# Coarser chunks in the first tile and finer chunks in the last tile of a split SiLU-and-multiply kernel

## The chip, the cores and the metric

One Trainium2 chip, one core. The metric is the device time of one execution in microseconds (us). The profile's span is about 2 us shorter than this time (468.4 against 470.3 us for the kernel before) and is what all positions below refer to.

## The reference

```python
batch, seq, dim = (32, 512, 2048)            # x: float32, 134.22 MB
x1, x2 = x[..., :1024], x[..., 1024:]
out = x1 * (1 / (1 + np.exp(-x1))) * x2      # float32, 67.11 MB
```

There are 16,384 rows. Each is read once (8 KB) and gives an output row of 4 KB.

## The kernel before

The rows are cut into 16 tiles of 128 partitions x 8 rows. Each tile is loaded by one 8 MB DMA from the SP queue, ScalarE (ACT) writes SiLU of the left half into an output tile, VectorE (DVE) multiplies the right half into it, and the output is stored from the ACT queue. There are two input and two output buffers. In the middle a tile is one SiLU, one multiply and one 4 MB store. The first tile is done in four chunks of 2 rows and written by five smaller stores; the last one in two chunks of 4 rows and written by two stores.

```python
K = 8
KC_EDGE = 2
KS = 4
OPENING = [
    (slice(0, None, 4), slice(0, 2)),      # 32 partitions, rows 0-1
    (slice(2, None, 4), slice(0, 4)),
    (slice(2, None, 4), slice(4, None)),
    (slice(0, None, 4), slice(2, None)),
    (slice(1, None, 2), slice(None)),      # 64 partitions, rows 0-7
]
in_pool = ctx.enter_context(tc.tile_pool(name="in_pool", bufs=2))
out_pool = ctx.enter_context(tc.tile_pool(name="out_pool", bufs=2))
...                                        # cut: load, silu, mul
load(0)
load(1)
for i in range(n_tiles):
    xt = loaded.pop(i)
    ov = view(out_flat, i)
    ot = out_pool.tile([P, K, half], dt, name="ot")
    if i < n_tiles - 1:
        kc = KC_EDGE if i == 0 else K
        for c in range(0, K, kc):
            silu(ot, xt, c, c + kc)
            mul(ot, xt, c, c + kc)
        for ps, ks in OPENING if i == 0 else [(slice(None), slice(None))]:
            nc.scalar.dma_start(out=ov[ps, ks], in_=ot[ps, ks])
        if i + 2 < n_tiles:
            load(i + 2)
        continue
    for c in range(0, K, KS):
        silu(ot, xt, c, c + KS)
        mul(ot, xt, c, c + KS)
    for c in range(0, K, KS):
        nc.scalar.dma_start(out=ov[:, c:c + KS], in_=ot[:, c:c + KS])
```

## Time and profile before

| | |
|---|---|
| time, first three runs | 470.42 us median (470.37 to 470.56) |
| time, with the three later runs | 470.39 us median (470.34 to 471.46) |
| share of the span: load queue, store queue | 66.4%, 33.2% of 16 DMA engines |
| share of the span: DVE, ACT | 30%, 24% |
| middle of the kernel | 435 GB/s |

Read the two DMA shares first: they add up to 99.6%. (The 16 engines move each DMA in packets. Packets that are issued and not yet moved wait in an engine's ring; together they are the backlog.) The end of the timeline (start, length, engine, line, operation, count, and in brackets how long the engine was idle and on what):

```profile
448.01 7.12 ACT L86 ACTIVATE ot<-xt 128x4096 f32<-128x4096 f32 x2 [17.20 <-DMA out_dram<-ot]
451.66 8.76 DVE L93 TENSOR_TENSOR ot<-ot,xt 128x4096 f32<-128x4096 f32 x2 [12.13 <-ACT ot L86]
456.12 4.67 ACTq L120 DMA_DIRECT2D out_dram<-ot  x2
```

The last tile waits for an output buffer (17.20 us, on the store that frees it), is computed from 448.01 on, and its first store goes out at 456.12, when the second half of the compute still runs.

### The profile page before, as it was taken

To read this page: it belongs to the slowest core of one execution; us is meant where nothing else is said; L and a number is where in the kernel's file an instruction comes from. 1 tells how busy PE (TensorE), PEld (TensorE's weight loads), DVE (VectorE), ACT (ScalarE), POOL (GpSimd) and SP (SyncE) were. 2 spreads that over 40 slices of the span, in tenths; PEclk is the share of its full clock that TensorE was granted. 3 is DMA by queue.
4 is the path that set the end of the run, shared out by engine and by line. 5 is a ranking of instruction groups with operands and counts; after the bars stand their busy time and mean duration, and the time that the engine had idled before them with its cause. 6 is when DMAs were issued, how large, how long until landed. Compare 5 with 4: busy or idle time off the path is not lost.

```text
span 468.4 us, 185 instructions
## 1 busy us (share of the span) xinstructions
DVE 139.3 (30%) x20; ACT 114.1 (24%) x21; POOL 0.2 (0%) x4
## 2 busy tenths in 40 slices
DVE  0070600704207042070520605116061150602543
ACT  1142305005050050601406014060230602306060
POOL 0000000000000000000000000000000000000000
DMA  9899999999999999999999999899999899999998
GB/s 442 364 470 425 448 403 403 493 403 403 448 465 431 403 442 409 493 403 414 437 448 448 403 448 465 386 448 439 411 493 442 372 439 493 403 448 403 428 423 358
DMA packets 4880, 201.33 MB, mean 430 GB/s; under 512 B 592, under 2 KB 592, under 8 KB 592
## 3 DMA queue, kind: packets, MB, share of 16 engines
q1 hardware_dynamic: 2304, 134.22, 66.4%
q10 hardware_dynamic: 2576, 67.11, 33.2%
HBM read 134.22 MB, written 67.11 MB: 430 GB/s over the span
## 4 chain that ended last, share of the span: by engine, by line
DMA 72%; DVE 14%; ACT 11%; DVEq 1%; issue 0%
DMA out_dram<-ot 63%; DVE ot L93 14%; ACT ot L86 11%; DMA xt<-in_x_dram 9%; DVEq L146 1%
## 5 line engine op out<-in xcount | busy, mean ns | idle before, releaser
L93 DVE TENSOR_TENSOR ot<-ot,xt 128x8192 f32<-128x8192 f32 (+2 forms) x20 | 139.3, 6983 | 321.1 <-ACT ot L86 321.1
L86 ACT ACTIVATE ot<-xt 128x8192 f32<-128x8192 f32 (+2 forms) x20 | 112.8, 5661 | 340.2 <-DMA out_dram<-ot 305.8
L86 ACT ACT_TABLE_LOAD x1 | 1.3, 1283 | 0.8 <-PEq L135 0.8
L135 POOL MEMSET const-bfloat16-1.0<- 128x1 bf16 x1 | 0.1, 102 | 0.0
L135 POOL MEMSET const-uint8-127<- 128x1 uint8 x1 | 0.1, 102 | 0.0
L135 POOL MEMSET const-float32-1.0<- 128x1 f32 x1 | 0.1, 99 | 0.0
L135 POOL MEMSET const-float32-0.0<- 128x1 f32 x1 | 0.1, 98 | 0.2 <-issue 0.2
## 6 DMA issues: line engine op xcount, KB each, us to landing
out_dram<-ot ACTq DMA_DIRECT2D x14, 4096.0 KB, 42.2
out_dram<-ot ACTq DMA_DIRECT2D x3, 2048.0 KB, 6.9
out_dram<-ot ACTq DMA_DIRECT2D x2, 512.0 KB, 17.6
out_dram<-ot ACTq DMA_DIRECT2D x1, 768.0 KB, 28.2
xt<-in_x_dram SPq DMA_DIRECT2D x16, 35.1
out_dram<-ot ACTq DMA_DIRECT2D x1, 256.0 KB, 11.3
```

What stands on the lines that cost most here:

```text
L86: nc.scalar.activation(out=ot[:, c:ce, :], in_=xt[:, c:ce, :half], func=mybir.ActivationFunctionType.Silu,)
L93: nc.vector.tensor_mul(out=ot[:, c:ce, :], in0=ot[:, c:ce, :], in1=xt[:, c:ce, half:],)
L135: nc = _bacc.Bacc("TRN2", target_bir_lowering=False, num_devices=1)
L146: with _tile.TileContext(nc) as tc:
```

## The change

Its intent: in the last tile, let the first store go out sooner by working in smaller pieces at first; in the first tile, save two small operations (one SiLU and one multiply, net) whose early results no store uses, since the last three stores need the last rows anyway.

```diff
-    KC_EDGE = 2
+    CHUNKS_EDGE = [2, 2, 4]
@@ the loop over tiles
-            kc = KC_EDGE if i == 0 else K
-            for c in range(0, K, kc):
+            c = 0
+            for kc in CHUNKS_EDGE if i == 0 else [K]:
                 silu(ot, xt, c, c + kc)
                 mul(ot, xt, c, c + kc)
+                c += kc
@@ the last tile
-        for c in range(0, K, KS):
-            silu(ot, xt, c, c + KS)
-            mul(ot, xt, c, c + KS)
+        c = 0
+        for kc in CHUNKS_EDGE:
+            silu(ot, xt, c, c + kc)
+            mul(ot, xt, c, c + kc)
+            c += kc
```

The stores are as before, so in the last tile the first one (rows 0 to 3) now waits for the second chunk and the other for the third.

## The prediction

> **What bounds the kernel now.** I read the page first, sections 1 to 3. The page shows how busy each engine is and whether the transfers ever pause:
>
> ```profile
> DVE 139.3 (30%) x20; ACT 114.1 (24%) x21; POOL 0.2 (0%) x4
> ...
> DMA  9899999999999999999999999899999899999998
> ...
> q1 hardware_dynamic: 2304, 134.22, 66.4%
> q10 hardware_dynamic: 2576, 67.11, 33.2%
> HBM read 134.22 MB, written 67.11 MB: 430 GB/s over the span
> ```
>
> The two compute engines work less than a third of the span. The load queue (q1) and the store queue (q10) together fill 66.4 + 33.2 = 99.6% of the 16 DMA engines' time. The change moves no byte, so it can only win time in which the DMA engines stand idle. At most 0.4% of the 468.4 us span, 1.9 us, is not packet time, and part of that is fixed start and end.
>
> The next question is where this idle time lies. I asked for the share of the DMA engines by stage; the columns are window, length, DVE busy, ACT busy, POOL busy, clock, DMA share, GB/s.
>
> ```profile
> 1.00:60.00 59.00, 17.59 (x5) 15.39 (x6) 0.00 (x0) 1.00 1.00 424
> 60.00:424.00 364.00, 104.30 (x12) 84.57 (x13) 0.00 (x0) 1.00 1.00 435
> ...
> 448.00:457.00 9.00, 5.34 (x2) 7.12 (x2) 0.00 (x0) 1.00 0.97 421
> 457.00:467.00 10.00, 3.42 (x1) 0.00 (x0) 0.00 (x0) 1.00 0.96 408
> ```
>
> The head is full, the middle is full, and only the last lines dip. The dips have to be read with care: a load packet of 64 KB takes 2.42 us and falls into the window in which it starts, so a window of 10 us can be off by several per cent. I therefore went to the single packet records of the trace near the end. They run without a break until the store of the last tile but one is through: on the first of the 16 engines its last packet ends at 456.85, on the last engine at 457.29. The next packet, the first of the last tile, starts between 456.97 and 457.30. So the idle time before it is 0.12 us on the earliest engine and 0.01 us on the latest. From there on packets of 16 KB follow each other every 0.61 us, the last one ends at 467.02, and 1.4 us of completion and closing barrier follow. That gap is all that a faster last tile can win.
>
> The chain of waits must be read against this. It ends so:
>
> ```profile
> 410.60 37.39 DMA out_dram<-ot
> ...
> 448.01 3.62 ACT ot L86
> ...
> 451.66 4.42 DVE ot L93
> 456.09 4.34 DVEq L146
> ```
>
> It looks as if the last tile's SiLU and multiply carried the end. They do not: the chain follows semaphores, and does not know that the DMA rings still hold the whole 4 MB store issued at 439.57. The compute of the last tile and that backlog run side by side, and they happen to end within 0.12 us of each other.
>
> The durations come from the groups by shape (columns: busy us, mean ns, idle before):
>
> ```profile
> L93 DVE TENSOR_TENSOR ot<-ot,xt 128x2048 f32<-128x2048 f32 x4 | 8.9, 2286 | 23.7 <-ACT ot L86 23.7
> L93 DVE TENSOR_TENSOR ot<-ot,xt 128x4096 f32<-128x4096 f32 x2 | 8.8, 4422 | 12.1 <-ACT ot L86 12.1
> L86 ACT ACTIVATE ot<-xt 128x2048 f32<-128x2048 f32 x4 | 7.3, 1897 | 19.7 <-DMA xt<-in_x_dram 19.7
> L86 ACT ACTIVATE ot<-xt 128x4096 f32<-128x4096 f32 x2 | 7.1, 3608 | 17.2 <-DMA out_dram<-ot 17.2
> ```
>
> **What the Trainium skill says.** "DMA: Bandwidth & Descriptors", section "Queues, rings and completion order", says that each DMA engine alternates between the queues that have work, a packet at a time. The trace agrees: in the middle a 64 KB load packet (2.42 us) and a 32 KB store packet (1.21 us) alternate on each engine. So who issues when changes the order of packets, not their sum, while any queue has work. The same page, "Where 436 GB/s comes from", puts the ceiling at 435 GB/s; the middle stage above runs at 435, so nothing is left there. "ScalarE: Activation LUTs", section "What ACT_TABLE_LOAD costs", gives an activation with immediates 186 ns + 0.833 ns an element and an overlap of 93 ns between neighbours. The trace agrees: 186 + 0.833 x 2048 = 1892 against 1897 measured, and the head's second SiLU starts at 23.570 while the first ends at 23.663. "VectorE: DVE Perf Modes", section "Side-by-side: where the cycles go for N=2048 bf16", counts about 150 cycles of setup beside the elements at 0.96 GHz; one element a cycle makes (2048 + 150) / 0.96 = 2290 ns against 2286 measured. So splitting an operation costs about 0.1 us on each engine.
>
> **The change, part by part.** Head, the first tile. Today's timeline (start, duration, engine):
>
> ```profile
> 21.75 5.51 ACT L86 ACTIVATE ot<-xt 128x2048 f32<-128x2048 f32 x3 [19.70 <-DMA xt<-in_x_dram]
> 23.70 8.90 DVE L93 TENSOR_TENSOR ot<-ot,xt 128x2048 f32<-128x2048 f32 x4 [23.70 <-ACT ot L86]
> 26.02 0.55 ACTq L112 DMA_DIRECT2D out_dram<-ot  x1
> 27.17 1.89 ACT L86 ACTIVATE ot<-xt 128x2048 f32<-128x2048 f32 x1
> 28.22 6.19 ACTq L112 DMA_DIRECT2D out_dram<-ot  x4
> 32.62 0.33 SPq L82 DMA_DIRECT2D xt<-in_x_dram  x1
> ```
>
> Chunks one and two stay as they are, and the first two stores need no other rows, so these are still issued at 26.02 and 28.22. Chunks three and four become one SiLU and one multiply of 4 rows. Removed: two SiLUs and two multiplies of 2 rows; added: one of each of 4 rows. The third SiLU started at 25.37 and will end at 25.37 + 3.61 = 28.98; its multiply runs 29.01 to 33.43, where today the fourth multiply ends at 32.59. The last three stores of this tile and the load of the third tile are thus issued 0.84 us later, at about 33.46. Does any queue run dry by it? The packet records say no. The second tile's load keeps q1 busy until 42.36, and the third tile's load only starts at 42.97, 10 us after it was issued; the third store is issued at 32.63 and gets its first packet at 45.38, 12.8 us later. A delay of 0.84 us disappears in either. Cost on the path: 0.
>
> Tail, the last tile. Removed: one SiLU and one multiply of 4 rows; added: two of each of 2 rows. SiLU one runs 448.01 to 449.91, its multiply 449.94 to 452.22; SiLU two ends at 451.72, and its multiply, gated by the multiply before it, ends at about 452.14 + 2.28 = 454.42. The first store needs both and goes out at 454.45 in place of 456.12: 1.67 us earlier. From issue to first packet it took 456.97 - 456.12 = 0.85 us, so its packets are ready by 455.30, while the older store holds the engines to 456.85. Of the 1.67 us, 0.12 us can be used on the earliest engine and 0.01 on the latest; the rest is waiting in the ring.
>
> The second half: SiLU three runs 451.63 to 455.24, its multiply 455.27 to 459.69 (today to 460.43), its store goes out at 459.72 and is ready at 460.57. The first half, 8 packets of 0.61 us an engine from 456.86 on, lasts until 461.75. So it is queued in time, as today (460.46 + 0.85 = 461.31 against 461.92). Gain: none.
>
> Sum: head 0, tail between -0.01 and -0.12 us, -0.07 as the middle. 470.42 - 0.07 = 470.35 us.
>
> **Rivals.** First, that the end of the last multiply sets the end of the kernel, as the chain of waits suggests. It comes 0.74 us earlier; a reader of that chain might even hope for the 1.67 us by which the first store goes out earlier. That would make 469.7 or 468.8 us. Against it: the unbroken packets from 456.97 to 467.02. I give it one chance in fifteen.
>
> Second, that the later issues in the head leave a hole, because the third tile's load and the large stores come 0.84 us late and all later tiles follow: 470.42 + 0.84 = 471.3 us. Against it: the 10 us of slack in q1. A weaker form is that the order of packets in the head shifts by one, so that the landing of the store which frees the last tile's output buffer (it starts the last SiLU at 448.01) moves by one load packet, 2.4 us. The new tail would then absorb a part: of the 2.4 us, 456.85 - 455.30 = 1.55 us is slack, and 0.85 would show, 471.3 us too. I see no reason for the shift, since the first two stores and the whole second load stand as they were. One in twenty.
>
> Third, that removing two small operations in the head and adding two in the tail costs or saves setup time. It is 0.1 us an operation on engines that idle two thirds of the time, so it makes no difference.
>
> **Range and chances.** The three runs of before spread over 0.19 us, 470.37 to 470.56; the expected gain is smaller than that. The range reaches 0.45 us to either side, which covers a part of the first rival's smaller form below and of the second rival above, and a chip that runs a little differently: 469.9 to 470.8. Two per cent is 9.4 us, five times all the idle time of the DMA engines, so faster by over 2% is practically excluded, and slower by as much would need a wait that nothing in the trace hints at: 0.005, 0.985 and 0.01.
>
> **What would show it.** Right: in the profile after, the third multiply of the head ends near 33.4, and the load behind it is issued there, but the second tile's SiLU still starts near 43.8 and the last tile's near 448.0; the first store of the last tile is issued near 454.4 and takes longer to land, about 8.0 us in place of 6.4 (462.5 - 454.45, since its packets hardly move); the last multiply ends near 459.7, and the span stays within 0.2 us of 468.4. Wrong: a span shorter by 0.7 us or more, with the packets ending earlier, would mean that the compute did carry the end; a last SiLU that starts later than 449.5 would mean that the head's delay travelled down the whole kernel.

## The result

| | before | after |
|---|---|---|
| time, median of 6 runs | 470.39 us | 470.28 us |
| range | 470.34 to 471.46 | 470.23 to 472.06 |
| five fastest of six | 470.34 to 470.56 | 470.23 to 470.48 |

The ratio is 1.0001, 95% interval 0.9984 to 1.0017: the same. A ratio is the mean time of one kernel's fast runs over that of the other's of the same rounds, so it is not quite the ratio of the medians quoted; here the single late runs, 472.06 us after and 471.46 us before, both enter.

The page of the changed kernel answers line by line to the one before. First busy time and queues:

```profile
DVE 139.5 (30%) x20; ACT 114.1 (24%) x21; POOL 0.2 (0%) x4
...
q1 hardware_dynamic: 2304, 134.22, 66.4%
q10 hardware_dynamic: 2576, 67.11, 33.2%
```

The shares of the queues are the same to the last digit. Now the stages, with the same columns as in the prediction:

```profile
1.00:60.00 59.00, 17.61 (x4) 15.30 (x5) 0.00 (x0) 1.00 1.00 425
...
448.00:457.00 9.00, 6.05 (x3) 7.22 (x3) 0.00 (x0) 1.00 0.97 417
457.00:467.00 10.00, 2.87 (x1) 0.00 (x0) 0.00 (x0) 1.00 0.96 411
```

In the tail stage 448 to 457 VectorE now does 6.05 us of work in place of 5.34, and after 457 only 2.87 in place of 3.42: the compute has moved forward, while the DMA columns hardly move. The head of the timeline after:

```profile
21.93 7.22 ACT L86 ACTIVATE ot<-xt 128x2048 f32<-128x2048 f32 x3 [19.88 <-DMA xt<-in_x_dram]
23.88 4.49 DVE L93 TENSOR_TENSOR ot<-ot,xt 128x2048 f32<-128x2048 f32 x2 [23.88 <-ACT ot L86]
26.20 9.21 ACTq L113 DMA_DIRECT2D out_dram<-ot  x5
29.18 4.43 DVE L93 TENSOR_TENSOR ot<-ot,xt 128x4096 f32<-128x4096 f32 x1 [0.81 <-ACT ot L86]
33.64 0.33 SPq L82 DMA_DIRECT2D xt<-in_x_dram  x1
```

and its end:

```profile
448.20 7.22 ACT L86 ACTIVATE ot<-xt 128x2048 f32<-128x2048 f32 x3 [17.17 <-DMA out_dram<-ot]
450.14 4.49 DVE L93 TENSOR_TENSOR ot<-ot,xt 128x2048 f32<-128x2048 f32 x2 [10.38 <-ACT ot L86]
454.66 5.58 ACTq L124 DMA_DIRECT2D out_dram<-ot  x2
455.44 4.43 DVE L93 TENSOR_TENSOR ot<-ot,xt 128x4096 f32<-128x4096 f32 x1 [0.81 <-ACT ot L86]
```

In this run the first tile landed 0.18 us later than in the one before (21.93 against 21.75), so subtract that. The head's last multiply then ends 0.84 us later (33.61 - 0.18 against 32.59) and the load behind it is issued 0.84 us later. The first store of the last tile goes out 1.64 us earlier (454.66 - 0.18 against 456.12). Both shifts are as computed. Neither arrives at the end: the packet records run through without the gap near 457 (before, it was 0.03 us on average over the 16 engines), and the last packets of the 16 engines end on average at 466.82 against 466.88 before. The latest engine, on which the end waits, ends at 467.22 against 467.02, because in this run one engine runs 0.2 us behind the fifteen others all through the last stages.

### The profile page after: what moved, and what is told of

Its sections match the earlier page's. It is cut to its first block, busy times and chain, and to the rows that moved or that the text cites. A ratio compares the mean times of both kernels' runs of the same rounds, so it can differ in the third digit from the quotient of the medians.

```text
span 468.6 us, 185 instructions
## 1 busy us (share of the span) xinstructions
DVE 139.5 (30%) x20; ACT 114.1 (24%) x21; POOL 0.2 (0%) x4
## 4 chain that ended last, share of the span: by engine, by line
DMA 72%; DVE 14%; ACT 12%; issue 0%
DMA out_dram<-ot 63%; DVE ot L93 14%; ACT ot L86 12%; DMA xt<-in_x_dram 9%
```

## The experiments

Two theories were to be told apart. The backlog theory: the DMA engines have work to the end, so compute at the edges can only cost time when it makes them run dry. The rival: the last multiply, or the head's delay, sets the end. The twelve runs below are of eleven kernels (one was run twice), each the changed kernel with its list of chunks split into HEAD and TAIL; the diffs are against that. The kernel before, run beside them, had a median of 470.28 to 470.33 us.

### Each half of the change alone

```diff
-    CHUNKS_EDGE = [2, 2, 4]
+    HEAD = [2, 2, 2, 2]     # as before
+    TAIL = [2, 2, 4]        # as changed
```

> The new tail (2, 2, 4) with the old head (2, 2, 2, 2). Backlog theory: the store of the last tile but one holds the DMA engines to about 456.9, so issuing the last tile's first store 1.5 to 1.7 us earlier wins at most 0.12 us: 470.2 to 470.5. Rival (the end of the last multiply sets the end): 0.7 us faster, 469.7.

Measured: 471.81, 470.75, 472.10, 470.39 us; ratio 1.0018 (1.0000 to 1.0036). This misses the expectation on the slow side, and it is not what the rival says either. The packet records of the profiled run (471.81) show why that one was late: fourteen engines end between 466.56 and 466.93, two at 467.59 and 468.12. The new tail can't have made these two late: they lag already when the sixth tile's load ends (154.39 and 155.08, the others by 153.89). I ran the same kernel again:

> The same kernel as tail_only, whose four runs spread from 470.4 to 472.1 and whose profiled run had two of the 16 DMA engines ending 0.7 and 1.2 us after the other fourteen. If that was a passing straggler: most runs at 470.2 to 470.5 as in the changed kernel. If the new tail with the old head brings it about: a median near 471.3 again.

Measured: 470.71, 471.58, 470.50, 470.60, 474.96, 470.82 us; ratio 1.0024 (0.9998 to 1.0049). The median, 470.76 us, lies between the two outcomes that were expected. The profiled run (470.71) has no straggler, all engines end between 466.68 and 467.07. So the late engines come and go, but a small part stayed in most runs: 470.5 to 470.8 and not 470.3 (one of the first four was at 470.39). The trace places it behind the last packet. In the closing barrier, where the engines wait for each other at the end of the program, ACT's last drain instruction starts at 468.35 and takes 118 ns, where in the kernel before it starts at 467.96 and takes 8 ns, and the barrier waits for it, about 0.3 us. Over all fourteen traces this late drain is there in exactly the four whose ACT stream has 65 instructions (both runs of this kernel and the two with an extra SiLU below), and in none of the ten with 64 or fewer. The full change has 64 like the kernel before: it adds one SiLU in the tail and takes one away in the head. That the length of the stream is the cause is suggested by this count, not shown.

```diff
-    CHUNKS_EDGE = [2, 2, 4]
+    HEAD = [2, 2, 4]        # as changed
+    TAIL = [4, 4]           # as before
```

> The new head (2, 2, 4) with the old tail (4, 4). Full-queue theory: the third tile's load is issued about 0.85 us later but had 10 us of slack, so 470.3 to 470.6. Rival (the head's delay travels down the kernel): 471.2 to 471.3.

Measured: 470.31 us median (470.29 to 470.35, four runs), ratio 0.9998 (0.9982 to 1.0015). The later load costs nothing.

### A coarser tail

```diff
-    TAIL = [2, 2, 4]
+    TAIL = [6, 2]
```

> Chunks of 6 and 2 rows in the last tile, head as in the changed kernel. The first store needs rows 0 to 3 and so the whole 6-row chunk: SiLU 5.3 + multiply 6.6 us from 448.0 on, issued at 459.9, first packet at 460.8. Backlog theory: the DMA engines stand idle from 456.9 to 460.8, so +3.5 to +3.9 us: 474.1. Rival (end of the last multiply, which moves from 460.4 to 462.1): +1.7 us, 472.1.

Measured: 473.99 us median (473.96 to 474.98), ratio 1.0081 (1.0066 to 1.0096). +3.7 us, as the backlog theory has it. (The profiled run was the late one, 474.98; in it one DMA engine ends the backlog at 458.19, 0.9 us behind the others, and the last tile starts 0.9 us late with it.)

```diff
-    TAIL = [2, 2, 4]
+    TAIL = [8]
```

> The last tile in one chunk of 8 rows. SiLU 7.0 + multiply 8.7 us from 448.0 on, both stores issued at 463.8, first packet at 464.65. Backlog theory: DMA idle from 456.9 to 464.65, +7.4 to +7.8 us: 478.0. Rival (end of the last multiply moves from 460.4 to 463.75): +3.3 us, 473.7.

Measured: 478.30 us median (478.17 to 479.34), ratio 1.0173 (1.0158 to 1.0188). +8.0 us against an expected 7.4 to 7.8. Its stages near the end (same columns) show the hole; first the kernel before, in the stage of the hole:

```profile
457.30:461.00 3.70, 3.12 (x1) 0.00 (x0) 0.00 (x0) 1.00 1.00 425
```

```profile
448.00:457.30 9.30, 2.05 (x1) 7.03 (x1) 0.00 (x0) 1.00 0.91 395
457.30:461.00 3.70, 3.70 (x1) 0.00 (x0) 0.00 (x0) 1.00 0.00 0
```

From 457.3 on VectorE is busy all the time and the DMA engines move nothing. The packet records give 7.7 us of idle time on average, up to the first packet at 464.82. The two runs settle what the tail's compute is worth: what counts is when the first store is ready, against the backlog's end at 457, and not when the last multiply ends. The rival's +1.7 and +3.3 us are out.

### How much slack the change bought

A useless SiLU of 2 rows, overwritten at once by the right one, delays the last tile in both kernels.

```diff
         c = 0
+        silu(ot, xt, 0, 2)
         for kc in TAIL:         # [4, 4] in the first kernel, [2, 2, 4] in the second
```

> The kernel before with one useless SiLU of 2 rows (1.82 us, overwritten by the right one) ahead of the last tile's first chunk. Backlog theory: the old tail has at most 0.12 us of slack, so nearly all of it shows: the first store's packets start at 458.8 and not at 457.0, +1.5 to +1.8 us, 472.0. Rival (end of the last multiply): +1.8 us, 472.2. Alone it doesn't tell them apart; it is the pair of the next run.

> The changed kernel with the same useless SiLU (1.82 us). Backlog theory: the new tail has 1.5 us of slack in the first store and about 1.2 us in the second, so only 0.2 to 0.6 us shows: 470.5 to 470.9, and the difference to the kernel before with the same SiLU is 1.1 to 1.6 us. Rival (end of the last multiply): the whole 1.8 us shows here too, and the difference is 0.1 to 0.7 us.

Measured with the old head and tail: 472.35, 472.29, 477.55, 474.99 us; with the new ones: 471.14, 471.24, 471.38, 471.15 us. The two slowest runs of the first kernel were not profiled and I cannot explain them, nor the single late runs of other kernels that were not profiled (472.06, 474.96 and 474.48 us among them; the kernel before has such runs too, up to 471.46). Its other two are 2.0 us over the kernel before, and the second kernel is 0.9 us over it. Both are about 0.3 us above what was expected (472.0, and the upper end of 470.5 to 470.9), and both have 65 ACT instructions and the late drain. The difference of the fastest runs, 1.15 us, lies in the range of the backlog theory. It leaves out the two slow runs; with all four the medians are 2.5 us apart. The packet records say the same without this scatter: the last packets end at 468.81 and 467.57, 1.24 us apart (the heads differ too, but both last tiles start near 448.0), the idle time before the last tile's stores is 1.9 us with the old tail, and 0.3 us before the first and 0.3 us before the second store with the new one. So the change does what it meant to; it buys some 1.3 us of slack, which the unchanged timing doesn't use.

### The tail without the backlog

The store of the last tile but one is left out. The result is wrong (4 MB of the output stay unwritten).

```diff
-                nc.scalar.dma_start(out=ov[ps, ks], in_=ot[ps, ks])
+                if i != n_tiles - 2:
+                    nc.scalar.dma_start(out=ov[ps, ks], in_=ot[ps, ks])
```

> The kernel before without the 4 MB store of the last tile but one (wrong on purpose: those rows of the output are not written). Backlog theory: the backlog is gone, the old tail's own path sets the end: SiLU at 448.0, first store's packets at 457.0, 9.8 us of packets; the same end as with the store, 470.3, although 9.7 us of DMA work is gone. A pure byte count would say 460.6.

> The changed kernel without the same store (wrong on purpose). Backlog theory: the engines are free when the new tail's first store comes: packets from 455.3, the second half ready at 460.56, after the first half's end at 460.2, end at 465.5: 469.0, about 1.3 us under the same cut of the kernel before. This is what the change is worth where no backlog hides it. Rival (end of the last multiply): 0.74 us between the two.

Measured: 470.38 us median (470.23 to 471.43) with the old edges; 469.00, 474.48, 470.76, 468.97 us with the new ones, too scattered (ratio 1.0010, 0.9959 to 1.0060). The profiled runs, 470.23 and 469.00 us, compare cleanly: the last packets end at 466.79 and 465.55, 1.24 us apart, where 1.3 was expected and the rival had 0.74. The stage in which the new tail's packets start earlier, first with the old edges, then with the new:

```profile
448.00:457.30 9.30, 5.79 (x2) 6.98 (x2) 0.00 (x0) 1.00 0.07 28
```

```profile
448.00:457.30 9.30, 6.61 (x3) 7.15 (x3) 0.00 (x0) 1.00 0.27 113
```

Two things follow. Taking 4 MB away from a kernel whose DMA engines are 99.6% busy won nothing with the old tail, because at this one place the compute of the last tile lies just as long beside it. And the change's 1.2 us shows in the profiled pair, where the backlog doesn't hide it (of the other runs, 470.39 and 470.37 against 468.97 us agree with it; the late ones, 471.43, 474.48 and 470.76, were not profiled).

### How far the head can be delayed

```diff
-    HEAD = [2, 2, 4]
+    HEAD = [8]
```

> The first tile in one chunk of 8 rows, tail as changed. The multiply ends at 21.8 + 7.0 + 8.7 = 37.5, so all stores of this tile and the third tile's load are issued there, 4.9 us later than in the kernel before, and the first store 11.5 us later. Full-queue theory: without stores between them the second tile's packets end at about 40.4, and the third tile's load is in the ring by then: 470.2 to 471.0. Rival (the head's delay travels down the kernel): 475.3.

Measured: 480.40, 480.09, 482.70, 482.38 us, ratio 1.0242 (1.0215 to 1.0269). Both theories miss, mine by some 10 us. The stage 99.5 to 106.8, first of the kernel before, then of this one:

```profile
99.50:106.80 7.30, 0.00 (x0) 1.98 (x1) 0.00 (x0) 1.00 0.98 422
```

```profile
99.50:106.80 7.30, 6.51 (x1) 0.29 (x1) 0.00 (x0) 1.00 0.00 0
```

The load of the third tile was indeed in the ring in time: at 40.9 no engine paused. The hole came 60 us later, and the timeline shows from where. The third tile's SiLU, first before, then with the head in one chunk:

```profile
75.85 7.03 ACT L86 ACTIVATE ot<-xt 128x8192 f32<-128x8192 f32 x1 [25.03 <-DMA out_dram<-ot]
```

```profile
90.26 7.03 ACT L87 ACTIVATE ot<-xt 128x8192 f32<-128x8192 f32 x1 [41.99 <-DMA out_dram<-ot]
```

It waits for the first tile's output buffer, and that came free 14.4 us later, since all five stores were issued from 37.7 on and follow one another: their first packet starts at 42.90 in place of 31.02, and the last store lands at 90.15 in place of 75.75. So the third tile's multiply ended at 106.0 in place of 91.6, and with it came the fifth tile's load. By then the store of the second tile had run out (last packet 99.48), and the engines stood idle for 8.0 us on average. The load packets that started again after the hole took longer than the 2.42 us of the others, 1.3 us in sum on each engine. Together that is 9.3 of the 9.8 us by which the span grew.

```diff
+            if i == 0:
+                silu(ot, xt, 0, K)     # with HEAD = [8]: the first tile's SiLU twice
```

> As the run with one chunk in the head, with the first tile's SiLU done twice (7.0 us more). The third tile's load is issued at 44.5. Full-queue theory: the second tile's packets end at about 40.4, so now there is a hole of 44.5 + about 1 to 1.5 - 40.4 = 5 to 5.6 us, and it stays to the end: 475.3 to 476.2. Rival (delay travels down the kernel whole): 470.4 + 11.9 = 482.3.

Measured: 486.87, 490.12, 486.86, 487.44 us, ratio 1.0372 (1.0341 to 1.0402). The hole that I expected is there, 5.4 us on average from 40.5 on; a second one of 8.4 us follows near 105, as in the run before. The number was wrong by that second hole and by some 2 us in which packets took longer.

To show that the output buffer, and not the late load, makes the hole, the next kernel leaves all compute as late as in the run with one chunk, but writes the first tile by one store. The five stores take 12 packets on each engine (2 + 2 + 2 + 2 + 4), one store takes 8, and each packet waits its turn behind a 64 KB load packet.

```diff
-            for ps, ks in OPENING if i == 0 else [(slice(None), slice(None))]:
+            for ps, ks in [(slice(None), slice(None))]:    # with HEAD = [8]
```

> The first tile in one chunk of 8 rows as before, but written by one 4 MB store in place of five. The two late issues (stores and third tile's load at 37.7) are the same as with five stores. Output-slot theory (formed after the run with one chunk): the hole at 99.5 to 106.9 came because the five stores take 12 turns of each DMA engine, so the first output buffer came free at 90.2 and not at 75.9, and the third tile's compute and the fifth tile's load with it. One store takes 8 turns: free at about 70.3, no hole, 470.2 to 471.0. Rival (the late issue of the third tile's load itself costs the time): as with five stores, 478 to 482.

Measured: 470.75 us median (470.69 to 470.88, five runs), ratio 1.0008 (0.9995 to 1.0021). The same two lines of this kernel:

```profile
71.57 7.03 ACT L87 ACTIVATE ot<-xt 128x8192 f32<-128x8192 f32 x1 [23.32 <-DMA out_dram<-ot]
```

```profile
99.50:106.80 7.30, 0.00 (x0) 6.22 (x1) 0.00 (x0) 1.00 1.04 449
```

With the load issued at 37.67, as late as before, the buffer comes free at 71.6, the DMA engines stay busy, and the time is back within 0.5 us of the kernel before. So a late load alone, and late stores alone, cost at most these 0.5 us; the hole needs the five stores to be both late and many, and the trace shows that it comes by the output buffer. No kernel with the right output that I ran is faster than the kernel before: the lowest medians are 470.28 us of the changed kernel and 470.31 us of the head alone, beside 470.28 to 470.39 us of the kernel before.

## Why the prediction was right

- **The bound.** DMA engines 99.6% full before and after; the measured 470.28 us against the predicted 470.35 us. Right; that the two agree to 0.07 us is luck, since runs of one kernel scatter by more. For the 435 GB/s the prediction names the Trainium skill, "DMA: Bandwidth & Descriptors", "Where 436 GB/s comes from". That section also says that a lower limit, about 358 GB/s, binds transfers between HBM and SBUF; the middle of this kernel ran at 435 GB/s, so here it did not bind.
- **The head: cost 0.** The shift of 0.84 us in the trace was exact, and the head alone measured 470.31 us. The conclusion is right, but the reason given was only half of it. I read the slack from the load queue, "10 us", and from the wait of the third store, "12.8 us", each by itself. The run with one chunk showed that the load did have its slack, and that a further limit lies behind it: when the first tile's last store lands and frees the output buffer. In the changed kernel this moved by 0.05 us (76.08 - 0.18 against 75.85), since the first packets of the stores only follow long after their issue. I had named this wait, but in the rival about the end of the kernel and not as a limit of the head.
- **The tail: 0.01 to 0.12 us.** The gap near 457 is gone in the trace, the mean end of the engines is 0.05 us earlier, and the medians differ by 0.11 us. The size was misread a little: 0.12 us compares the earliest end with the earliest start; over all engines the gap was 0.03 us on average, and none on the latest engine, on which the end waits. So the expected gain was nearer to 0 than to 0.07 us. All of this is inside the scatter of the runs, so the sign of the gain is not shown by the times. What is shown is the mechanism: the pairs with the extra SiLU and without the store bring out 1.24 us each in the packet records, which the backlog hides.
- **The forecast of the trace.** First store of the last tile at 454.5 when the 0.18 us are taken off (454.4 predicted), its landing after 8.05 us (8.0 predicted), the last multiply's end at 459.69 with the same correction (459.7 predicted), span 468.6 us (468.2 to 468.6 predicted).
- **The rivals.** The end of the last multiply as the bound is refuted by the tails of 6 + 2 and 8 rows. The delay that travels down the kernel is refuted for 0.84 us by the head alone; when the output buffer comes free 14 us late it is real, by another path than the rival said. Its weaker form, a shift by one load packet, can be seen in the late profiled run of the new tail with the old head: the third tile's SiLU starts at 78.28, 2.4 us late, and the fourth's only 1.0 us late, as much as its slow engines lag. Setup times of small operations: on the engines they showed nowhere; but an added ACT instruction does go with 0.3 us in the closing barrier, which neither side had.

## What to carry to other kernels

When the DMA queues are full, ask of each edge only whether the engines run dry: compare when the new work is ready with when the backlog ends, and take only the difference. The chain of waits doesn't show that backlog, for it follows semaphores. In a double-buffered stream, follow both buffers: a late load has the slack of the load queue, but stores that are both late and finely cut hold their output buffer longer and can open a hole several tiles later.

## What the Trainium skill lacked or had wrong

- "DMA: Bandwidth & Descriptors", "Latency and other measured facts", gives about 600 ns to the first byte on these queues. Here, with the engines idle, it was 0.84 to 0.85 us for a store from ACT, from the start of the issuing instruction to the first packet, in each of five traces (the tails of 6 + 2 and 8 rows, both kernels without the store, the old tail with the extra SiLU; for example 463.98 to 464.82), of which 0.34 us is that instruction; from its end it is 0.5 us. The first load from SP took 1.0 us in the same way. The page doesn't say from where it counts.
- The same page, "Queues, rings and completion order", has the alternation by packet, but not what follows from unequal packets: by turns alone a store of 8 KB packets gets at most 8 / (8 + 64), one ninth, of an engine's bytes beside 64 KB loads (an estimate from the packet sizes in the trace). The first tile's output in packets of 8 to 32 KB held its buffer until 90.2, in packets of 32 KB until 71.6, both issued from 37.7 on.
- No page has the slow first packets of some loads: after 8.0 us of idle time they took up to 4.4 us in place of 2.42, 1.3 us in sum on each engine; the very first load of the kernel lost about 0.6 us in the same way. Idle time is not the only cause: in the run with one store the third tile's first load packets, at 40.2, took up to 3.6 us (1.1 us in sum) though no engine had paused. The cause stays open.
- No page has a late closing drain on ACT: 118 to 133 ns and about 0.3 us late in all four traces with 65 ACT instructions, 8 ns and on time in all ten with fewer.
